# The seam before the up-projection of a decoder layer on one Trainium2 core: buffers of the first weight pairs exchanged, the last rows handled ahead of splits, one operand split by halves, gate sums in two groups

## The chip, the cores and the metric

The kernel runs on one core of a Trainium2 chip. A core has five engines that work side by side and meet through semaphores: TensorE (PE in the profile), VectorE (DVE), ScalarE (ACT), GpSimd (POOL) and SyncE (SP), which here issues most of the loads. The metric is the device time of one execution in microseconds (us). The kernel before took 1789.0, 1787.13 and 1788.75 us in three runs, a median of 1788.75.

## What is computed

One layer of a decoder trunk in float32, 1024 tokens of width 1024. Three branches (a recurrence, an attention, a cross-attention) are gated, projected and added to `x`; a feed-forward block with a causal convolution of width 3 follows. Cut to what matters here:

```python
def conv_ffn(x, g, w_up, conv_w, conv_b, w_down):
    h = rms_norm(x, g) @ w_up
    t = h.shape[1]
    hp = jnp.pad(h, ((0, 0), (CONV_W - 1, 0), (0, 0)))
    acc = conv_b + hp[:, 0:t] * conv_w[0]
    for i in range(1, CONV_W):
        acc = acc + hp[:, i:i + t] * conv_w[i]
    gate, val = jnp.split(acc, 2, axis=-1)
    return (jax.nn.silu(gate) * val) @ w_down

def reference(x, ...):
    ...
        x = x + merged @ w_out[l]
        x = x + conv_ffn(x, norm2_g[l], w_up[l], conv_w[l], conv_b[l], w_down[l])
    return x
```

`w_up` is 1024 x 5632 (2816 gate and 2816 value columns), `w_down` 2816 x 1024.

## The kernel before

**Matmuls in parts.** Each float32 operand is split into a high part (`hi`, a copy on ACT in a narrower form) and a low part (`lo`, what the copy lost, a subtraction). A product is then the sum of three: high times high, high times low, low times high. So each operand costs one ACT instruction and one subtraction, on DVE or POOL, before PE can use it. In `hl` (weights) the copy is line 1483 and the subtraction, always on POOL, line 1486. For the activations they are lines 1391 (ACT) and 1396 (DVE, or POOL where `eng=nc.gpsimd` is given). On PE all these matmuls are line 119, and the plain ones and the transposes line 105.

**Seven products for eight.** The up-projection multiplies 2 x 2 blocks of `w_up` with 2 x 2 blocks of the normed activations in Winograd's form: seven products in place of eight, of sums and differences of blocks. A product is four contraction tiles of 128 by three combinations of parts: 12 matmuls of 128 x 128 by 128 x 512, in one PSUM bank. Its activation sides have the names `11`, `21`, `22`, `T4`, `T1`, `T2`, `T3`, for the products 1 to 7 in this order (`side`, line 1468). Each side is two tiles (halves of the contraction, `j` = 0 and 1), each in a high and a low part. In the profile, the sides are `B` (11, 21, 22) and `BT` (T1 to T4), the tensors that they are split from `A`, `raw` and `t`.

**The seam.** `out_proj` computes `x + merged @ w_out` by row tiles of 128 tokens, norms each (`norm`: line 1342 loads the rows of x, 1347 adds, 1348 squares, 1354 scales), transposes it (`spread`, line 105) and forms the sums of blocks (`sums`, line 1378). The last row tile, the seventh, is left to `up_phase`, which does the first products between the pieces that still lack it. `old` is the part of a side that the first three of four row tiles of a half fill (384 of 512 columns), `new` the last 128. A split over both contraction halves of `old` has 768 elements to a partition in a tile, one of `new` 256.

**Pairs.** `w_up` is worked off in 22 pairs of blocks, gate and value columns in turn. Two tiles of 128 x 1024 are loaded for a pair by `load(n)` (line 1479), in buffers with the tag `rw` for even pairs and `wr` for odd ones, two buffers each; `t2`, the tensor from which the side T2 is split, lies in the buffers `wr` until it is split. `prep1`, `prep2` and `prep3` form the weight sides on POOL: sums of the blocks (lines 1505, 1506, 1518, 1519) and the splits by `hl`. Pair 0's weights are loaded and partly split earlier (`early`, the names `wsec`, `wsum`, `qk`).

**Products and what follows them.** `step(n, i)` does product i of pair n, and what reads its bank: `p1` is a copy of product 1's bank (line 1585), lines 1608, 1617, 1618, 1627 and 1634 on DVE add or subtract banks into the tiles `u`, which hold the up-projection with two columns of padding. `step(0, ..)` of product 7 is written out at lines 1696 to 1700. `conv` does the convolution on ACT (line 1552) and DVE (1553, 1554), and the gate: a sigmoid on ACT (1557) and products on DVE (1558 for the gate columns, 1563 for the value columns, which give `gall`). After each value pair, `act_sums` forms the sums that the down-projection's seven products need: two sums with `late` false and two with `late` true, all at line 1571, and sends `gall` and the sums to the DRAM tensor `actd` from ACT's queue (lines 1576, 1580, 1581).

**What sets the order.** PE's instructions, and all that is wrapped in `pinned` or `keep_in_program_order`, stay in the order in which the code writes them; the rest is placed by a scheduler with its own estimates, engine by engine. On the chip each engine then works strictly in its order.

The order of the products at the seam is (0,1), (1,1), the transposes of the last row tile, (0,2), (1,2), (0,5), (0,6), (0,7), (0,4), (0,3), where (n,i) is pair n's product i. Then come (1,6), (1,5), (1,4), (1,7), (2,1), (1,3), for pair 2 the products 5, 6, 2, 7, 4, 3, and for each later pair 1, 5, 6, 2, 7, 4, 3. Products 5 and 3 of a pair add into one bank, so do 6 and 7, and 1 and 2: before product 3 starts, DVE must have read product 5's sum (line 1618; 1700 for pair 0). Pair 3's product 1 follows (2,3). It is the down-projection (`down_phase`) that ends the kernel; its first loads take the buffers `rw` (`draw`) and `wr`.

Of the kernel before, what the change touches and what calls it, by code (L numbers as in the profile page):

```python
# [15 lines left out]
ALU = mybir.AluOpType  # L16
# [4 lines left out]
C = 64  # L21
# [28 lines left out]
class Trunk:  # L50
# [1407 lines left out]
    def up_phase(self, raws, t2, operand, split_hi, split_lo, sums, norm, spread):  # L1458
        nc = self.nc
        old, new = slice(0, 384), slice(384, 512)  # L1460
# [9 lines left out]
        pairs = [(o + 2 * f, f, o > 0) for f in range(NF // 2) for o in (0, NF)]  # L1470
        W, st = {}, {}

        def load(n):
            if n < len(pairs):
                tag, m = ("rw", pairs[n][0]) if n % 2 == 0 else ("wr", pairs[n][0])
                pool = self.pool_r if n % 2 == 0 else self.pool_wt
                W[n] = [pool.tile([128, 1024], F32, name=self.nm(tag), tag=tag, bufs=2) for _ in range(2)]
                for i in range(2):
                    nc.sync.dma_start(W[n][i], self.I["w_up"][m + i])

        def hl(src, pool, tags, n=1024, keep=False, queue=False):
            hi, lo = (pool.tile([128, n], F32R, name=self.nm(t), tag=t, bufs=16 if t == "l4" else 2) for t in tags)
            ins = nc.scalar.activation(hi, src, AF.Copy)  # L1483
            if keep:
                self.pinned(ins)
            ins = nc.gpsimd.tensor_tensor(lo, src, hi.bitcast(F32), ALU.subtract)  # L1486
            if queue:
                self.tc.keep_in_program_order(ins)
            return hi, lo

        L, R = slice(0, 512), slice(512, 1024)
# [5 lines left out]
        def prep2(n):  # L1497
            if n == 0:
                w = self.early[1]
            else:  # L1500
                w1, w2 = W[n]
                s = self.t4("it")
                st[n, "s"] = s
                fix = self.tc.keep_in_program_order if n == 2 else lambda ins: ins
                fix(nc.gpsimd.tensor_tensor(s[:, L], w2[:, L], w2[:, R], ALU.add))
                fix(nc.gpsimd.tensor_tensor(s[:, R], s[:, L], w1[:, L], ALU.subtract))
                w = hl(s, self.pool_l, ("l4", "l4"))
            st[n, 5], st[n, 6] = [[x[:, c] for x in w] for c in (L, R)]

        def prep3(n):  # L1510
            if n == 0:
                w2, s4 = self.early[2], self.early[3][:, R]
            else:
                w1, w2 = W.pop(n)
                s = st.pop((n, "s"))
                s4 = self.pool_r.tile([128, 512], F32, name=self.nm("s4"), tag="s4", bufs=1)
                fix = self.tc.keep_in_program_order if n == 1 else lambda ins: ins
                fix(nc.gpsimd.tensor_tensor(w2[:, L], w1[:, L], w2[:, L], ALU.subtract))
                fix(nc.gpsimd.tensor_tensor(s4, w1[:, R], s[:, R], ALU.subtract))
            w = hl(w2, self.pool_wt, ("wh", "wl"), keep=n == 1, queue=n == 1)  # L1520
            st[n, 7], st[n, 4] = [[x[:, c] for x in w] for c in (L, R)]
            if n == 1:
                return s4
            if n:
                st[n, 3] = hl(s4, self.pool_l, ("l4", "l4"), 512)
# [21 lines left out]
        L2, R2 = slice(2, 514), slice(514, 1026)  # L1547
# [35 lines left out]
        def evacuate(n):  # L1583
            p1 = st[n, "p1"] = self.r4("p1", n=512)
            ins = nc.scalar.activation(p1, st[n, "A"], AF.Copy)
            if n < 2:
                self.pinned(ins)

        def step(n, i):
# [10 lines left out]
            elif i == 5:  # L1600
                C = st[n, "C"] = bank()
                product(n, 5, C, True, True)
            elif i == 6:
# [3 lines left out]
                    st[n, "u1"] = u_tile()  # L1607
                self.pinned(nc.vector.tensor_tensor(st[n, "u1"][:, R2], Bk, st[n, "p1"], ALU.add))
                if n and pairs[n - 1][2]:
                    if n == 2:  # L1610
                        act_sums(pairs[n - 1][1], False)
                    act_sums(pairs[n - 1][1], True)
            elif i == 7:
                Bk = st.pop((n, "B"))
                product(n, 7, Bk, False, True)
                v = st[n, "u2"] = u_tile()
                nc.vector.tensor_tensor(v[:, L2], Bk, st.pop((n, "p1")), ALU.add)
                nc.vector.tensor_tensor(v[:, R2], st[n, "C"], v[:, L2], ALU.add)
            elif i == 40:
                Dk = st[n, "D"] = bank()  # L1620
                product(n, 4, Dk, True, True)
# [32 lines left out]
        prep1(1)  # L1654
        hi("22", old)
        hi("T1", old, (0,))
        hi("T2", old)
        next(norm)
        lo("T1", old, (0,))
        next(norm)  # L1660
        hi("T1", old, (1,))
        lo("T2", old)
        lo("22", old, eng=nc.gpsimd)
        step(0, 1)
        evacuate(0)
        next(norm, None)
        st[1, "A"] = bank()
        product(1, 1, st[1, "A"], True, True)
        spread()
# [4 lines left out]
        lo("T1", js=(1,))  # L1674
        hi("T2", new)
        lo("T2", new)
        load(1)
        step(0, 2)
        hi("T3", old)
        step(1, 2)  # L1680
        prep3(0)
        sums(384, 512, (1,))
        lo("T3", old)
        hi("T3", new)
        lo("T3", new)
        hi("22", new)
        lo("22", new, eng=nc.gpsimd)
        operand("T4", self.pool_a, "A", bufs=4)
        hi("T4")
        lo("T4")  # L1690
        prep2(0)
        st[0, 3] = hl(self.early[3][:, R], self.pool_l, ("l4", "l4"), 512, True)
        step(0, 5)
        prep2(1)
        step(0, 6)
# [370 lines left out]
```

## Time and profile before

| | us |
|---|---|
| median of three runs | 1788.75 |
| the profiled execution | 1788.76 |
| its span, first to last instruction | 1787.0 |
| PE busy (10479 matmuls) | 1771.8 |
| DVE busy | 1181.5 |
| ACT busy | 865.3 |
| POOL busy | 792.5 |
| mean granted clock of PE | 0.999 |

The profile is one execution, recorded by the hardware. Busy time is that in which an engine works on an instruction. PE is the engine that is hardly ever idle, so time goes where PE waits or where the clock granted to it is below 1. In the rows, `L1396` is a line of the kernel, `out<-in` are the program's names without their numbers, `128x512` a tile's partitions and elements, `x4` the number of instructions in a group. The bracket `[0.90 <-DVE BT L1396]` says that the engine stood idle for 0.90 us before this row, and what let it go.

### The profile page before, as it was taken

What the parts mean: (1) busy time and instruction counts of PE and PEld (TensorE: products, weight loads), DVE (VectorE), ACT (ScalarE), POOL (GpSimd) and SP (SyncE); (2) the same over time, 40 slices, a digit from 0 to 9 for tenths busy, and PEclk for the clock granted to TensorE, in tenths of its full rate; (3) what the DMA queues carried; (4) which work ended last, traced back from release to release, by engine and by line L of the source; (5) the groups of instructions that cost most, each with busy time, mean ns of one, the idle gap of its engine ahead of it and who ended that gap; (6) DMA issues with size and microseconds to landing.
All of it is one profiled execution on the core that took longest, in us unless ns stands there. A gap on an engine that the chain in (4) does not pass through costs nothing.

```text
span 1787.0 us, 27327 instructions
## 1 busy us (share of the span) xinstructions
PE 1771.8 (99%) x10479; PEld 1440.1 (81%) x10479; DVE 1181.5 (66%) x1604; ACT 865.3 (48%) x1566; POOL 792.5 (44%) x448
## 2 busy tenths in 40 slices
PE   9999999999999999999999999999999999999999
PEld 7777778888888888777777888878888888888887
DVE  5667774898988624234443962687767777795597
ACT  6544343656666635534444334544444445454343
POOL 3223352331231453122332542487677677545454
PEclk9999999999999999999999999999999999999999
DMA  5145565111112443568554553223323323386476
GB/s 210 60 161 182 179 224 163 51 54 57 54 57 77 127 120 95 212 226 282 201 190 177 203 186 110 103 99 103 111 89 99 119 90 121 126 317 220 146 239 209
DMA packets 122771, 261.28 MB, mean 146 GB/s; under 512 B 28681, under 2 KB 43657, under 8 KB 122514
## 3 DMA queue, kind: packets, MB, share of 16 engines
q1 hardware_dynamic: 85026, 193.83, 32.9%
q10 hardware_dynamic: 33840, 53.10, 8.1%
q0 software_dynamic: 3776, 12.62, 2.4%
q8 instruction: 82, 1.34, 0.3%
q14 instruction: 47, 0.39, 0.1%
HBM read 178.99 MB, written 80.48 MB: 145 GB/s over the span
## 4 chain that ended last, share of the span: by engine, by line
PE 81%; DVE 6%; POOL 2%; issue 1%; ACT 1%; DMA 1%; DVEq 0%; SPq 0%; POOLq 0%; ACTq 0%
PE mm L119 66%; PE g L119 12%; PE g L105 3%; DVE it L554 1%; DVE at L939 1%; DVE inst L556 1%; DMA A<-yd 1%; POOL wl L1486 0%; DVE gall L1571 0%; DMA scr<-at 0%; POOL hf L781 0%; DVE w L344 0%; POOL l L1486 0%; DVE w L834 0%; DVE qk L877 0%
## 5 line engine op out<-in xcount | busy, mean ns | idle before, releaser
L81 POOL TENSOR_TENSOR wl<-wr,wh 128x1024 fp32r<-128x1024 f32 (+2 forms) x78 | 197.1, 2527 | 468.0 <-ACT wh L80 465.0
L119 PE MATMUL mm<-xhi,wh 128*128 128x512 f32 x784 | 260.3, 413 | 0.5 <-DVE w L331 0.4
L119 PE MATMUL mm<-xlo,wh 128*128 128x512 f32 x784 | 243.6, 392 | 0.0
L119 PE MATMUL mm<-xhi,wl 128*128 128x512 f32 x784 | 242.5, 391 | 0.0
L119 PEld LDWEIGHTS mm<-xlo,wh 128*128 128x128 f32 x784 | 147.1, 188 | 33.3 <-DVE xlo L208 0.4
L119 PEld LDWEIGHTS mm<-xhi,wl 128*128 128x128 f32 x784 | 147.0, 188 | 33.1 <-POOL wl L81 0.7
L119 PEld LDWEIGHTS mm<-xhi,wh 128*128 128x128 f32 x784 | 136.7, 190 | 28.9 <-issue 6.1
L80 ACT ACTIVATE wh<-wr 128x1024 fp32r<-128x1024 f32 (+2 forms) x78 | 81.8, 1049 | 130.9 <-PE mm L119 100.1
L119 PE MATMUL mm<-dw,da 128*128 128x512 f32 x528 | 120.3, 389 | 0.0
L119 PE MATMUL mm<-BT,l 128*128 128x512 f32 x504 | 118.0, 389 | 1.4 <-POOL l L1486 1.4
L1775 POOL TENSOR_TENSOR dw<-draw,dw 128x512 fp32r<-128x512 f32 x55 | 82.6, 1511 | 75.7 <-ACT dw L1773 70.0
L119 PEld LDWEIGHTS mm<-dw,da 128*128 128x128 f32 x528 | 99.1, 188 | 20.6
L119 PEld LDWEIGHTS mm<-BT,l 128*128 128x128 f32 x504 | 94.5, 188 | 21.5 <-POOL l L1486 1.8
L119 PE MATMUL mm<-BT,wh 128*128 128x512 f32 x352 | 108.7, 389 | 0.9 <-DVE BT L1396 0.9
L119 PE MATMUL mm<-B,wh 128*128 128x512 f32 x352 | 108.8, 390 | 0.0
L939 DVE TENSOR_TENSOR_SCAN at<-at,nrt 128x128 f32<-128x128 f32 (+3 forms) x64 | 96.3, 1514 | 18.2 <-ACT at L933 18.0
L1774 DVE TENSOR_TENSOR da<-draw,da 128x512 fp32r<-128x512 f32 x77 | 64.2, 839 | 51.5 <-ACT da L1772 51.2
L1486 POOL TENSOR_TENSOR l<-it,l 128x1024 fp32r<-128x1024 f32 x21 | 50.9, 2422 | 90.2 <-ACT l L1483 90.1
L119 PE MATMUL g<-dw,da 128*128 128x512 f32 x396 | 90.2, 389 | 0.0
L119 PEld LDWEIGHTS g<-dw,da 128*128 128x128 f32 x396 | 74.3, 188 | 15.4
L1772 ACT ACTIVATE da<-draw 128x512 fp32r<-128x512 f32 x77 | 48.2, 628 | 78.5 <-PE mm L119 32.0
L834 DVE TENSOR_TENSOR w<-w,nrt 128x1024 f32<-128x1024 f32 x24 | 46.6, 1941 | 57.3 <-ACT w L833 46.4
(337 smaller groups left out, 3979.2 us busy)
## 6 DMA issues: line engine op xcount, KB each, us to landing
wr<-in_w_in_dram SPq DMA_DIRECT2D x48, 512.0 KB, 3.6
draw<-actd SPq DMA_DIRECT2D x77, 256.0 KB, 2.9
draw<-in_w_down_dram SPq DMA_DIRECT2D x55, 256.0 KB, 4.6
at<-scr SPq DMA_DIRECT2D x24, 512.0 KB, 6.0
wr<-in_w_up_dram SPq DMA_DIRECT2D x22, 512.0 KB, 3.5
actd<-gall ACTq DMA_DIRECT2D x44, 256.0 KB, 3.2
rw<-in_w_up_dram SPq DMA_DIRECT2D x20, 512.0 KB, 3.5
gsd<-w ACTq DMA_DIRECT2D x18, 512.0 KB, 3.0
```

The lines of the kernel that those rows point to most:

```text
L80: (fix_hi or fix)(self.nc.scalar.activation(hi, raw, AF.Copy))
L81: fix(self.nc.gpsimd.tensor_tensor(lo, raw, hi.bitcast(F32), ALU.subtract))
L105: self.pinned(self.nc.tensor.transpose(out, in_, self.ident[:n, :n]))
L119: self.pinned(self.nc.tensor.matmul(*a, **k))
L554: self.pinned(nc.vector.tensor_tensor(tv, X[:, 0:s, s : s + 1].to_broadcast([128, s, n]), X[:, s : s + 1, s + 1 : 64].to_broadcast([128, s ...
L556: self.pinned(nc.vector.tensor_tensor(X[:, 0:s, s + 1 : 64], X[:, 0:s, s + 1 : 64], tv, ALU.add))
L834: fix(nc.vector.tensor_tensor(g, g, self.nrb, ALU.mult))
L939: self.pinned(nc.vector.tensor_tensor_scan(sn[:, :W][:, ::-1], sn[:, :W][:, ::-1], self.nrt[:, 1152 - W :][:, ::-1], 1.0, ALU.mult, ALU.max))
L1486: ins = nc.gpsimd.tensor_tensor(lo, src, hi.bitcast(F32), ALU.subtract)
L1772: self.pinned(nc.scalar.activation(A[:, 0], a, AF.Copy))
L1774: self.pinned(nc.vector.tensor_tensor(A[:, 1], a, A[:, 0].bitcast(F32), ALU.subtract))
L1775: nc.gpsimd.tensor_tensor(Wt[:, 1], w, Wt[:, 0].bitcast(F32), ALU.subtract)
```

## The change

All edits are in `up_phase`. The even pairs now have the buffers `wr` and the odd ones `rw`; pair 1 is loaded earlier, in `rw`, in the order of the program. The last row tile's squares and scaling stand ahead of several splits, whose halves are reordered. T3's low parts are split half by half. The low half of `wsum` and pair 1's sums come in a fixed order on POOL. After pair 2's product 6 only two gate sums of pair 1 are done; the other two come behind the second addition after pair 2's product 7.

```diff
         def load(n):
             if n < len(pairs):
-                tag, m = ("rw", pairs[n][0]) if n % 2 == 0 else ("wr", pairs[n][0])
-                pool = self.pool_r if n % 2 == 0 else self.pool_wt
+                tag, m = ("wr", pairs[n][0]) if n % 2 == 0 else ("rw", pairs[n][0])
+                pool = self.pool_wt if n % 2 == 0 else self.pool_r
                 W[n] = [pool.tile([128, 1024], F32, name=self.nm(tag), tag=tag, bufs=2) for _ in range(2)]
                 for i in range(2):
-                    nc.sync.dma_start(W[n][i], self.I["w_up"][m + i])
+                    ins = nc.sync.dma_start(W[n][i], self.I["w_up"][m + i])
+                    if n == 1:
+                        self.pinned(ins)
...
-                fix = self.tc.keep_in_program_order if n == 2 else lambda ins: ins
+                fix = self.tc.keep_in_program_order if n < 3 else lambda ins: ins
...
-            w = hl(w2, self.pool_wt, ("wh", "wl"), keep=n == 1, queue=n == 1)
+            w = hl(w2, self.pool_wt, ("wh", "wl"), keep=n < 2, queue=n < 2)
...
                 if n and pairs[n - 1][2]:
-                    if n == 2:
-                        act_sums(pairs[n - 1][1], False)
-                    act_sums(pairs[n - 1][1], True)
+                    act_sums(pairs[n - 1][1], n > 2)
             elif i == 7:
...
-                nc.vector.tensor_tensor(v[:, R2], st[n, "C"], v[:, L2], ALU.add)
+                ins = nc.vector.tensor_tensor(v[:, R2], st[n, "C"], v[:, L2], ALU.add)
+                if n == 2:
+                    self.pinned(ins)
+                    act_sums(pairs[n - 1][1], True)
...
         hi("T1", old, (0,))
-        hi("T2", old)
         next(norm)
+        load(1)
         lo("T1", old, (0,))
+        hi("T2", old, (0,))
         next(norm)
-        hi("T1", old, (1,))
-        lo("T2", old)
+        lo("T2", old, (0,))
         lo("22", old, eng=nc.gpsimd)
         step(0, 1)
+        next(norm, None)
+        hi("T2", old, (1,))
         evacuate(0)
-        next(norm, None)
+        hi("T1", old, (1,))
+        lo("T2", old, (1,))
         st[1, "A"] = bank()
...
-        load(1)
         step(0, 2)
+        prep3(0)
         hi("T3", old)
         step(1, 2)
-        prep3(0)
         sums(384, 512, (1,))
-        lo("T3", old)
         hi("T3", new)
-        lo("T3", new)
+        for j in range(2):
+            for ts in (old, new):
+                lo("T3", ts, (j,))
         hi("22", new)
         lo("22", new, eng=nc.gpsimd)
         operand("T4", self.pool_a, "A", bufs=4)
+        st[0, 3] = hl(self.early[3][:, R], self.pool_l, ("l4", "l4"), 512, True, True)
         hi("T4")
         lo("T4")
         prep2(0)
-        st[0, 3] = hl(self.early[3][:, R], self.pool_l, ("l4", "l4"), 512, True)
         step(0, 5)
```

The order of PE's instructions is the same before and after. The places that matter are on DVE and POOL. In these rows an instruction stands with its line, its operation, out<-in and its tile; lines behind 1479 have moved by two or three numbers in the kernel after.

On DVE, the low parts of T3 and then of T4. `BT_1_0_10523` and `BT_1_1_10524` are T3's low parts for the contraction halves 0 and 1, of `old` (384 columns) and `new` (128); `BT_1_0_10667` and `BT_1_1_10668` are T4's. The difference, with + for the kernel after:

```order
 L1396 TENSOR_TENSOR BT_1_0_10523<-A_9819,BT_0_0_10521 128x2x384
+L1396 TENSOR_TENSOR BT_1_0_10523<-A_9819,BT_0_0_10521 128x2x128
 L1396 TENSOR_TENSOR BT_1_1_10524<-A_9820,BT_0_1_10522 128x2x384
-L1396 TENSOR_TENSOR BT_1_0_10523<-A_9819,BT_0_0_10521 128x2x128
 L1396 TENSOR_TENSOR BT_1_1_10524<-A_9820,BT_0_1_10522 128x2x128
 L1396 TENSOR_TENSOR BT_1_0_10667<-raw_9818,BT_0_0_10665 128x1024
 L1396 TENSOR_TENSOR BT_1_1_10668<-raw_9818,BT_0_1_10666 128x1024
```

The first half's second piece has moved ahead of the second half's first piece.

On DVE, the gate sums between the two products 6 and 7 of pair 2; L1608, L1617, L1618 and L1627 are the reads of PSUM banks described above, and before stands:

```order
L1544 MEMSET u_10957 128x2
L1608 TENSOR_TENSOR u_10957<-mm_10944,p_1643_10891 128x512
L1571 TENSOR_TENSOR gall<-gall 128x512 x4
L1544 MEMSET u_11005 128x2
L1617 TENSOR_TENSOR u_11005<-mm_10944,p_1643_10891 128x512
L1618 TENSOR_TENSOR u_11005<-mm_10927,u_11005 128x512
L1627 TENSOR_TENSOR u_11005<-u_11005,mm_11009 128x512
L1553 SCALAR_TENSOR_TENSOR g_11024<-u_11005,params,g_11024 128x512
L1553 SCALAR_TENSOR_TENSOR g_11030<-u_11005,params,g_11030 128x512
```

and after, where the lines behind 1618 are three further down and the sums are at L1573:

```order
L1546 MEMSET u_10957 128x2
L1610 TENSOR_TENSOR u_10957<-mm_10944,p_1643_10891 128x512
L1573 TENSOR_TENSOR gall<-gall 128x512 x2
L1546 MEMSET u_11001 128x2
L1617 TENSOR_TENSOR u_11001<-mm_10944,p_1643_10891 128x512
L1618 TENSOR_TENSOR u_11001<-mm_10927,u_11001 128x512
L1573 TENSOR_TENSOR gall<-gall 128x512 x2
L1630 TENSOR_TENSOR u_11001<-u_11001,mm_11009 128x512
L1637 TENSOR_TENSOR u_10957<-mm_10927,u_10957 128x512
L1555 SCALAR_TENSOR_TENSOR g_11024<-u_11001,params,g_11024 128x512
```

Of the four sums two now stand behind L1618, and the addition behind product 3 (L1637, before L1634) stands ahead of the convolution.

On POOL, from pair 0's split of `wsec` to pair 1's sums (`wsum` is pair 0's too; `it`, `s` and the raw weights `wr` or `rw` are pair 1's; `B` is side 22's low part); before:

```order
L1486 TENSOR_TENSOR wl_10648<-wsec_10307,wh_10647 128x1024
L1396 TENSOR_TENSOR B_1_0_10511<-A_9821,B_0_0_10509 128x2x128
L1396 TENSOR_TENSOR B_1_1_10512<-A_9822,B_0_1_10510 128x2x128
L1505 TENSOR_TENSOR it_10690<-wr_10612 128x512
L1506 TENSOR_TENSOR it_10690<-it_10690,wr_10611 128x512
L1486 TENSOR_TENSOR l_1607_10674<-wsum_10308,l_1606_10673 128x512
L1486 TENSOR_TENSOR l_1611_10694<-it_10690,l_1610_10693 128x1024
L1518 TENSOR_TENSOR wr_10612<-wr_10611,wr_10612 128x512
L1519 TENSOR_TENSOR s_1619_10755<-wr_10611,it_10690 128x512
L1486 TENSOR_TENSOR wl_10759<-wr_10612,wh_10758 128x1024
```

and after:

```order
L1488 TENSOR_TENSOR wl_10631<-wsec_10307,wh_10630 128x1024
L1396 TENSOR_TENSOR B_1_0_10511<-A_9821,B_0_0_10509 128x2x128
L1396 TENSOR_TENSOR B_1_1_10512<-A_9822,B_0_1_10510 128x2x128
L1488 TENSOR_TENSOR l_1607_10670<-wsum_10308,l_1606_10669 128x512
L1507 TENSOR_TENSOR it_10690<-rw_10539 128x512
L1508 TENSOR_TENSOR it_10690<-it_10690,rw_10538 128x512
L1488 TENSOR_TENSOR l_1611_10694<-it_10690,l_1610_10693 128x1024
L1520 TENSOR_TENSOR rw_10539<-rw_10538,rw_10539 128x512
L1521 TENSOR_TENSOR s_1619_10755<-rw_10538,it_10690 128x512
L1488 TENSOR_TENSOR wl_10759<-rw_10539,wh_10758 128x1024
```

The low half of `wsum` stands ahead of the two sums `it`, and the sums read `rw` in place of `wr`. On SP the load of the last rows of `x` (L1342) now stands ahead of the first of the two loads into the next pair's weight buffers, where it stood behind it.

## The prediction

> **What bounds the kernel now.** The page's first part gives PE 1771.8 of 1787.0 us busy, so a change can only win where PE stands still. The view of waits, kept to PE, has only five of them in the stretch that the diff touches; its columns are the waiting engine and line, the releaser, total, count, longest.
>
> ```profile
> PE mm L119 <- DVE u L1618: 2.2, 1, 2.2
> PE mm L119 <- POOL l L1486: 1.4, 1, 1.4
> PE mm L119 <- DVE BT L1396: 0.9, 1, 0.9
> PE g L105 <- ACT sq L1354: 0.6, 1, 0.6
> PE mm L119 <- ACT l L1483: 0.4, 1, 0.4
> ```
>
> The timeline of PE sets them in time: start, duration, line, tile, shape, count, and in brackets the idle time with its releaser.
>
> ```profile
> 1163.18 0.39 PE L119 MATMUL mm<-BT,wh 128*128 128x512 f32 x1
> 1164.47 0.50 PE L119 MATMUL mm<-BT,wh 128*128 128x512 f32 x1 [0.90 <-DVE BT L1396]
> ...
> 1186.83 2.88 PE L119 MATMUL mm<-B,l 128*128 128x512 f32 x12
> ...
> 1191.59 5.32 PE L119 MATMUL mm<-BT,l 128*128 128x512 f32 x22 [1.42 <-POOL l L1486]
> ...
> 1204.68 0.39 PE L119 MATMUL mm<-BT,wl 128*128 128x512 f32 x1
> 1207.30 4.32 PE L119 MATMUL mm<-B,l 128*128 128x512 f32 x12 [2.23 <-DVE u L1618]
> 1211.42 0.92 PE L119 MATMUL mm<-B,wh 128*128 128x512 f32 x2
> 1212.17 0.40 PE L119 MATMUL mm<-B,wl 128*128 128x512 f32 x1
> ...
> 1214.48 2.88 PE L119 MATMUL mm<-BT,l 128*128 128x512 f32 x12
> ```
>
> A product is 12 matmuls. At 1186.83 they take 2.88, the last of them 0.39, so one starts every (2.88 - 0.39) / 11 = 0.227 us and a product takes 2.72. At 1207.30 a product takes 4.12 (to 1211.42), and the next 3.06 (to 1214.48): 1.40 + 0.34 = **1.74 us lost to the clock**. The windows of PE (stretch, its length, busy time with count, granted clock, DMA share, GB/s) show it:
>
> ```profile
> 1207.00:1208.00 1.00, 0.70 (x3) 1.00 0.68 258
> 1209.00:1210.00 1.00, 1.00 (x4) 0.50 0.00 0
> ```
>
> So the change plays for 5.6 us of waits (2.2 + 1.4 + 0.9 + 0.6 + 0.4, rounded values) and 1.74 of slow clock; each wait also costs some 0.2 us more than its figure (1164.47 - 1163.18 - 0.23 = 1.06 for the 0.90). That makes about 8.4 us at most, 1780.4. The times of before are those of the profiled execution, 1788.76 (span 1787.0 and 1.76 around it), which is the median, 1788.75, to 0.01.
>
> **The last rows of x.** Start, duration and line again, of SP, DVE, ACT and PE:
>
> ```profile
> 1141.84 0.43 SPq L1342 DMA_DIRECT2D x<-in_x_dram  x1
> 1146.29 1.29 DVE L1347 TENSOR_TENSOR x<-mm,x 128x512 f32<-128x512 f32 x2 [0.45 <-DMA x<-in_x_dram]
> 1150.12 1.15 ACT L1354 ACTIVATE sq<-x,ss 128x1024 f32<-128x1024 f32 x1 [0.54 <-POOL ss L180]
> 1150.29 0.39 PE L119 MATMUL mm<-B,wl 128*128 128x512 f32 x1
> 1151.32 1.09 PE L105 MATMUL g<-kon,sq 128*128 128x128 f32 x8 [0.65 <-ACT sq L1354]
> ```
>
> The transposes start at 1151.32 and could at 1150.52 (1150.29 + 0.23): 0.80. The load no longer stands behind a weight load on SP, and DVE waits for it 0.45 us; the squares and the scaling on ACT now also stand ahead of T2's and T1's splits. 0.45 of an earlier load and about 0.4 of reordering cover it: **-0.80** (bounds 0 and -0.80). It is worth something only if what follows is earlier too.
>
> **T3 by halves, and POOL beside it.** Rows of DVE, then POOL:
>
> ```profile
> 1147.50 0.95 DVE L1396 TENSOR_TENSOR BT<-raw,BT 128x768 fp32r<-128x768 f32 x1
> 1159.85 0.41 DVE L1378 TENSOR_TENSOR A<-A,A 128x256 f32<-128x256 f32 x1
> 1161.19 3.56 DVE L1396 TENSOR_TENSOR BT<-A,BT 128x768 fp32r<-128x768 f32 x4
> 1164.68 3.44 DVE L1396 TENSOR_TENSOR BT<-raw,BT 128x1024 fp32r<-128x1024 f32 x2
> ```
> ```profile
> 1161.77 2.37 POOL L1396 TENSOR_TENSOR B<-A,B 128x256 fp32r<-128x256 f32 x2 [2.12 <-ACT B L1391]
> 1165.47 1.56 POOL L1505 TENSOR_TENSOR it<-wr 128x512 f32<-128x512 f32 x1 [1.34 <-DMA wr<-in_w_up_dram]
> 1167.11 2.16 POOL L1506 TENSOR_TENSOR it<-it,wr 128x512 f32<-128x512 f32 x1
> 1169.24 1.28 POOL L1486 TENSOR_TENSOR l<-wsum,l 128x512 fp32r<-128x512 f32 x1
> ```
>
> T3's four low parts (768, 768, 256, 256 elements) take 3.56 where 0.95 and 0.41 apiece would give 2.72. The first half needs the third of them now and will need the second: the 0.90 (1.06 with its edge) goes for that matmul. But the rows show a second thing: **an elementwise DVE instruction with all operands in SBUF and a POOL instruction hold each other up**. The sum `it` at 1167.11 takes 2.16 beside a split of DVE, and a POOL instruction of that shape takes 1.28 when DVE works from PSUM (1169.24). The Trainium skill, SBUF — State Buffer, section "Who interferes with whom", says that the loser of the port pair which the two share is blocked wholly, not slowed; the rows agree (2.16 against 1.28), and without that rule the sum would be the third rival's.
>
> Before, POOL stood idle 1.34 us here for the load into `wr`. Now pair 1 is in `rw`, loaded early, and the low half of `wsum` is ahead of the sums: POOL has three instructions ready as soon as its two splits `B` are done, just when DVE has four of six pieces left. The six alone are 2 x 0.95 + 2 x 0.41 + 2 x 1.27 (an estimate, 0.95 x 4/3) = 5.3; from 1161.19 they ended at 1168.12 (1164.68 + 3.44), 6.9 later. With five POOL instructions between them (about 0.6 of each `B`, 1.28 + 1.30 + 1.30) they take up to 5.3 + 5.1 = 10.4. Less the 0.80 of an earlier start, T4's last piece is done between 1167.3 (as before) and 1170.8; I take 1169.4, since most of the instructions ready will take turns: **+1.3** for T4. So PE loses about 0.9 to 1.3 us at each of T3's second half, T4's two halves and product (0,3): the waits are spread out, not gone.
>
> **What follows 1:1.** ACT and POOL, the chain behind T4:
>
> ```profile
> 1178.63 1.20 ACT L1557 ACTIVATE sg<-g 128x512 f32<-128x512 f32 x2 [1.71 <-DVE g L1554]
> 1180.42 1.30 POOL L1486 TENSOR_TENSOR l<-s,l 128x512 fp32r<-128x512 f32 x1 [1.71 <-ACT l L1483]
> 1208.15 4.74 POOL L1486 TENSOR_TENSOR wl<-wr,wh 128x1024 fp32r<-128x1024 f32 x2
> ```
>
> The convolution of pair 0 (DVE L1553, L1554) comes behind T4's pieces on DVE, ACT's gates behind it, ACT's `l<-s` behind those, and POOL waits for that at 1180.42. From there POOL never stops until the stretch ends, so its 1.3 goes straight through: product (2,5), which waits for POOL at 1191.59, starts at 1192.9 (**+1.3**).
>
> **Gate sums by twos.** DVE:
>
> ```profile
> 1198.93 6.88 DVE L1571 TENSOR_TENSOR gall<-gall 128x512 f32<-128x512 f32 x4
> 1206.46 0.69 DVE L1618 TENSOR_TENSOR u<-mm,u 128x512 f32<-128x512 f32 x1
> 1238.56 1.42 DVE L1571 TENSOR_TENSOR gall<-gall 128x512 f32<-128x512 f32 x2
> ```
>
> Beside POOL the four sums take 1.72 each (alone 0.71, at 1238.56), and L1618, which reads the bank into which product (2,3) adds, stands behind all four. Two of them go behind it: 3.4 earlier, against the 2.39 that PE lost (1207.30 - 1204.68 - 0.23). So that wait goes: product (2,3) starts at 1191.59 + 1.3 + 13.3 = 1206.2 (13.3 from 1191.59 to 1204.91) and ends at 1208.9. A sum moved behind L1618 delays L1627 by 1.4 to 3.4; that costs PE nothing, since its reader, the convolution, has no PE work behind it for several products, and 1.4 to 3.4 if that cover were gone.
>
> **What is late next.** Product (3,1) takes its low weights from the first of the two `wl` splits at 1208.15, which ends at half of 4.74, 1210.5; its third matmul needs them and ran at 1212.17, behind the slow clock. Now the split ends at 1210.5 + 1.3 = 1211.8, and PE comes to that matmul at 1208.9 + 0.45 = 1209.4: **a new wait of about 2.5 us**, on POOL in place of DVE. Behind it on PE stand the rest of (3,1) and the products 5 and 6 of pair 3; ACT's copy of (3,1)'s bank waits with them, and nothing that PE needs in the next two products waits for that copy. Ten matmuls later, at 1211.8 + 2.3 = 1214.1, the product is done, against 1214.48: the sum is **-0.3** where the clock stays full, 1788.4. With the slow clock again, 1.74 on top: **+1.4**, 1790.2.
>
> Which? A 2.23 us wait dropped the clock to 0.50; a 1.42 us wait did not. A 2.5 us wait is nearest to the first. Of the three times shown, 1789.0, 1787.13 and 1788.75, one is lower by 1.6 to 1.9, the size of the 1.74: I read it as a run without the drop, so two runs in three have it, and a median has it likelier still. The Trainium skill, TensorE: Matmul & The Clock Gate, section "What's actually happening", has the clock fall only after an idle window of about 3.4 us, and by that neither wait would touch it: the sum would be 1788.4. The trace disagrees with its 0.50 after 2.23 us.
>
> **At nothing.** The exchange of `rw` and `wr` in the later pairs moves no wait of PE; at the end the first loads of the down phase wait for pair 21's splits, at the latest as the two `wr` loads did before, and their first reader comes 18 us later (1573.80 - 1549.99 - 5.82). That is the cover, and what they'd cost beyond it is their lateness.
>
> ```profile
> 1549.99 5.82 SPq L1749 DMA_DIRECT2D wr<-in_w_down_dram  x2
> 1573.80 6.51 PE L119 MATMUL mm<-dw,da 128*128 128x512 f32 x28
> ```
>
> **Rivals.**
> - Forecast, 46%: POOL's split takes DVE's place and the clock drops: 1790.2 (1789.5 to 1791.5).
> - Same wait, clock full, 23%: 1788.4. For it: one of three runs, the 1.42 wait; against: the row of 0.50.
> - DVE and POOL take fewer turns, 20%: T4 is done up to 1.9 sooner than before (5.3 from 1160.9, which is 1161.19 less part of the 0.80, to 1166.2), so all behind it too: third matmul of (3,1) at 1210.5 - 1.9 = 1208.6, product done 1210.9, -3.6 with a full clock: 1785.2; with the drop 1786.9. Against: 2.16 and 1.72 in the rows.
> - POOL's split is in time as well and all waits go, 5%: 1780.4 to 1784. Against: POOL has no idle time from 1180.42 on.
> - Slower, 6%: the turns cost more than my 10.4 allows (each T4 piece also behind ACT's high part). It decides at T4 done 3.4 later than before, 1171.5: -0.3 + 2.1 + 1.74 = +3.5; at 1172.2, 1793.
> - The change doesn't do what it says: if the sums stay late, PE waits for DVE as now and 1.3 later, 1790.0: inside the forecast.
>
> **How the numbers follow.** 1790.2 is the likeliest. The range leaves out the case in which all goes and the slower one: 1785.2 to 1791.8. Faster by over 0.2% (3.6 us, about what a measurement of this kernel tells from no change), under 1785.2: the 5%, and a third of the third: 0.12. Slower, over 1792.3: 0.06. Within: 0.82.
>
> **What would show it.** The list of PE's waits loses DVE L1618 and ACT sq, and gains POOL `wl` at 2 to 3 us near 1209; DVE BT waits several times for about 1 us; POOL's `l<-s` near 1180.4 stands about 1.3 later; the window behind the new wait shows 0.50. Wrong would be: `l<-s` earlier than 1180 (third rival), no wait of PE on POOL (fourth), or one on another line.

## The result, and the profile after

| | before | after |
|---|---|---|
| median of 17 runs, us | 1788.02 | 1790.83 |
| lowest and highest | 1786.24, 1790.78 | 1789.56, 1793.19 |
| ratio, 95% interval | | 1.0016 (1.0009 to 1.0022) |
| profiled execution (span) | 1788.76 (1787.0) | 1793.19 (1791.4) |

The kernel is slower by 1.6 to 3.9 us (0.09% to 0.22% of 1788): the change moves time rather than saving any. The profiled execution of after happens to be the slowest of the 17, so its rows need a correction, which comes below.

The list of PE's waits, after (in all, times, longest; groups of under 0.7 us left out, and those outside the seam but for the one on L1610):

```profile
PE mm L119 <- POOL wl L1488: 2.5, 1, 2.5
PE mm L119 <- DVE BT L1396: 2.3, 3, 1.2
PE mm L119 <- DVE u L1610: 1.9, 1, 1.9
...
PE mm L119 <- POOL l L1488: 1.5, 1, 1.5
...
PE mm L119 <- DVE u L1706: 0.7, 1, 0.7
```

ACT's `sq` and DVE's L1618 are gone; POOL's `wl`, two more waits on `BT`, one on L1706 and one on L1610 have come. PE's timeline sets them in time:

```profile
1149.53 0.39 PE L119 MATMUL mm<-B,wl 128*128 128x512 f32 x1
1149.76 1.03 PE L105 MATMUL g<-kon,sq 128*128 128x128 f32 x8
...
1164.93 0.49 PE L119 MATMUL mm<-BT,wh 128*128 128x512 f32 x1 [1.17 <-DVE BT L1396]
1167.16 0.50 PE L119 MATMUL mm<-BT,wh 128*128 128x512 f32 x1 [0.57 <-DVE BT L1396]
1169.39 0.50 PE L119 MATMUL mm<-BT,wh 128*128 128x512 f32 x1 [0.57 <-DVE BT L1396]
...
1206.11 2.88 PE L119 MATMUL mm<-B,l 128*128 128x512 f32 x12
1211.90 0.50 PE L119 MATMUL mm<-B,wl 128*128 128x512 f32 x1 [2.45 <-POOL wl L1488]
1215.62 5.88 PE L119 MATMUL mm<-BT,l 128*128 128x512 f32 x24
...
1359.77 0.72 PE L119 MATMUL mm<-BT,wh 128*128 128x512 f32 x2 [1.89 <-DVE u L1610]
```

The transposes follow the matmul before them without a gap (1149.76 - 1149.53 = 0.23). Product (2,3) starts at 1206.11 at full speed. Product (3,1) then waits 2.45 us for POOL, and the window behind it has the clock at half:

```profile
1213.00:1215.00 2.00, 2.00 (x6) 0.50 0.74 246
```

Rows of DVE, then of POOL, for the other end of the chain:

```profile
1157.00 2.63 DVE L1378 TENSOR_TENSOR raw<-t,raw 128x256 f32<-128x256 f32 x1
...
1160.22 4.66 DVE L1396 TENSOR_TENSOR BT<-A,BT 128x768 fp32r<-128x768 f32 x4
1164.80 4.53 DVE L1396 TENSOR_TENSOR BT<-raw,BT 128x1024 fp32r<-128x1024 f32 x2
```
```profile
1156.72 2.63 POOL L1488 TENSOR_TENSOR wl<-wsec,wh 128x1024 fp32r<-128x1024 f32 x1 [3.70 <-ACT wh L1485]
...
1162.60 1.99 POOL L1488 TENSOR_TENSOR l<-wsum,l 128x512 fp32r<-128x512 f32 x1
1164.56 1.46 POOL L1507 TENSOR_TENSOR it<-rw 128x512 f32<-128x512 f32 x1
1166.10 2.15 POOL L1508 TENSOR_TENSOR it<-it,rw 128x512 f32<-128x512 f32 x1
...
1181.65 1.29 POOL L1488 TENSOR_TENSOR l<-s,l 128x512 fp32r<-128x512 f32 x1 [1.70 <-ACT l L1485]
```

The six pieces on DVE now take from 1160.22 to 1169.33 (1164.80 + 4.53), 9.1 us in place of 6.9; between them stand POOL's three, each slower than the 1.3 us that such an instruction takes without DVE beside it. `l<-s`, which starts POOL's long stretch, is at 1181.65 against 1180.42.

**Where the profile's 4.4 us lie.** PE's instructions have the same order in both, so their starts can be set against each other. At the matmul ahead of the transposes after is 0.76 us *ahead* (1149.53 against 1150.29); that difference arose far ahead of the seam, where both kernels issue the same work. At the end of product (3,1) after is 1.14 behind (1215.62 against 1214.48): the seam costs **1.9** to that point, and 0.27 more within the next products, whose first matmuls still run with the slow clock. At 1224 another 0.4 comes, behind a gate product on DVE that waits for ACT until 1222.94; at 1359.77 there are 2.2, and some 0.4 near the end. The 2.2 are not the seam's, as the last section shows.

### The profile page after: what moved, and what is told of

Read it like the earlier page. It is cut to its first block, busy times and chain, and to the rows that moved or that the text cites. A ratio compares the mean times of both kernels' runs of the same rounds, so it can differ in the third digit from the quotient of the medians.

```text
span 1791.4 us, 27323 instructions
## 1 busy us (share of the span) xinstructions
PE 1772.0 (99%) x10479; PEld 1439.2 (80%) x10479; DVE 1183.7 (66%) x1604; ACT 864.1 (48%) x1566; POOL 792.8 (44%) x448
## 4 chain that ended last, share of the span: by engine, by line
PE 79%; DVE 6%; POOL 3%; issue 2%; ACT 1%; DMA 1%; DVEq 0%; POOLq 0%; SPq 0%; ACTq 0%
PE mm L119 64%; PE g L119 12%; PE g L105 3%; POOL l L1488 1%; DVE it L554 1%; DVE at L939 1%; DVE inst L556 1%; POOL wl L1488 1%; DMA A<-yd 1%; POOL it L1507 0%; DMA scr<-at 0%; POOL it L1508 0%; POOL hf L781 0%; DVE w L344 0%; DVE w L834 0%
## 5 line engine op out<-in xcount | busy, mean ns | idle before, releaser
L1554 ACT ACTIVATE g<-u,params 128x512 f32<-128x512 f32 x88 | 65.1, 770 | 40.4 <-DVE u L1637 24.0
```

Source lines behind the costliest of these rows:

```text
L1554: nc.scalar.activation(c, u[:, 2 + h * 512 : 514 + h * 512], AF.Identity, scale=self.par("cw2", m), bias=self.par("cb", m))
```

## The experiments

The ratio of each is to the kernel before, run beside it.

**Gate sums alone.** The kernel before with this edit only:

```diff
-                    if n == 2:
-                        act_sums(pairs[n - 1][1], False)
-                    act_sums(pairs[n - 1][1], True)
+                    act_sums(pairs[n - 1][1], n > 2)
...
-                nc.vector.tensor_tensor(v[:, R2], st[n, "C"], v[:, L2], ALU.add)
+                ins = nc.vector.tensor_tensor(v[:, R2], st[n, "C"], v[:, L2], ALU.add)
+                if n == 2:
+                    self.pinned(ins)
+                    act_sums(pairs[n - 1][1], True)
```

> The kernel before, with the gate sums by twos and nothing else of the change. Theory (DVE's place is taken by POOL): the 2.2 us wait on L1618 goes, and product (3,1) waits about 2.4 us for the first of pair 3's splits on POOL, which ends at about 1210.5 as before; product (3,1) ends 0 (clock at 0.50 again) to 1.6 us (clock full) sooner: ratio to the kernel before 0.9990 to 1.0002. Rival (the gate sums were the whole loss and POOL is in time): 4 us less, ratio 0.9978. Rival (the gate sums are what makes the change slower): ratio 1.001 or more.

Measured: 1.0006 (0.9998 to 1.0015), no difference that the interval can tell. PE's timeline:

```profile
1210.04 0.79 PE L119 MATMUL mm<-B,wl 128*128 128x512 f32 x1 [2.51 <-POOL wl L1486]
```

The DVE wait of 2.23 us went and one of 2.51 on POOL took its place. The ratio is a little over the theory's 1.0002, which lies inside its interval. The rival of 4 us less is out; the one of 1.001 or more is not excluded by the interval, but no row speaks for it: the only new wait stands in the place of the old one.

**Gate sums undone.** The change without that edit (the diff above, backwards).

> The whole change with the four gate sums back ahead of L1618. Theory: T4 is done as late as in the changed kernel (about 1.2 us behind the kernel before, 1.9 against the entry into the seam), POOL's split at 1180 with it, so the sums on DVE start at 1200.1 and L1618 is done at about 1208.5; PE waits there some 2.2 us with the slow clock behind it, and the POOL split at 1211.9 is hidden: the end is within 0.5 us of the changed kernel, ratio to the kernel before 1.0013 to 1.0020. Rival (the turns of DVE and POOL at T4 cost nothing, the sums do): ratio 0.9995 to 1.0003.

Measured: 1.0014 (1.0005 to 1.0023), within the theory's range. PE waits 2.28 us for the read behind the four sums; the slow clock that was expected behind it did not come in the profiled execution (1.00). So the slowness comes with the rest of the change, not with the sums.

**Buffers back.** The change with `rw` and `wr` as before:

```diff
-                tag, m = ("wr", pairs[n][0]) if n % 2 == 0 else ("rw", pairs[n][0])
-                pool = self.pool_wt if n % 2 == 0 else self.pool_r
+                tag, m = ("rw", pairs[n][0]) if n % 2 == 0 else ("wr", pairs[n][0])
+                pool = self.pool_r if n % 2 == 0 else self.pool_wt
```

> The whole change with the buffers as before: pair 1 in wr, pair 2 in rw; the load of the last rows stands behind an rw load again. Theory: POOL waits for the wr load again and takes fewer turns with DVE, so T4 is done about 1168.1 or earlier, PE's waits at T3 and T4 shrink, and POOL's split for product (3,1) comes about 1.5 us sooner than in the changed kernel: ratio to the kernel before 0.9998 to 1.0008. Rival (the exchange costs nothing; the order of POOL and the halves do): ratio 1.0015.

Measured: 1.0019 (1.0010 to 1.0028). The theory missed: POOL's rows are those of after, to the hundredth in duration.

```profile
1162.40 1.99 POOL L1488 TENSOR_TENSOR l<-wsum,l 128x512 fp32r<-128x512 f32 x1
1164.36 1.46 POOL L1507 TENSOR_TENSOR it<-wr 128x512 f32<-128x512 f32 x1
1165.90 2.15 POOL L1508 TENSOR_TENSOR it<-it,wr 128x512 f32<-128x512 f32 x1
```

With `l<-wsum` ahead of the sums, the load into `wr` is there before POOL comes to them. The exchange neither causes the turns nor costs anything that shows; that is the rival.

**T3 whole.** The change with T3's low parts in the old order:

```diff
+        lo("T3", old)
         hi("T3", new)
-        for j in range(2):
-            for ts in (old, new):
-                lo("T3", ts, (j,))
+        lo("T3", new)
```

> The whole change with T3's low parts in the old order (768, 768, 256, 256 elements). Theory: the halves only move the wait inside product (0,7): its second matmul waits about 1.4 us in place of none, its seventh about 0.2 in place of 1.2, and T4's last piece is done at 1169.3 as in the changed kernel, so nothing behind changes: ratio to the kernel before 1.0010 to 1.0020. Rival (the halves cause the extra turns with POOL): T4 done 1 us or more earlier, ratio 1.0006 or less.

Measured: 1.0018 (1.0010 to 1.0027), as the theory has it. PE waits 1.44 us at the second matmul of product (0,7), in place of 1.17 at the seventh, and T4's pieces end at 1169.22 (1164.69 + 4.53). The halves are worth nothing here.

**The high half of `wsum` behind T4's.** One ACT instruction moved back, the only difference to after:

```diff
-        st[0, 3] = hl(self.early[3][:, R], self.pool_l, ("l4", "l4"), 512, True, True)
         hi("T4")
+        st[0, 3] = hl(self.early[3][:, R], self.pool_l, ("l4", "l4"), 512, True, True)
         lo("T4")
```

> The whole change with one ACT instruction moved: the high half of wsum behind T4's high parts, as before the change. POOL's order is kept, so POOL waits for it and starts its three instructions at about 1164.7 in place of 1162.6. Theory (turns of DVE and POOL make T4 late): DVE's T3 pieces run alone, T4's last piece is done at about 1167.1 in place of 1169.3, POOL's split at 1181.65 comes about 2 us sooner, and with it product (2,5) and (3,1): 2 us less than the changed kernel, ratio to the kernel before 1.0000 to 1.0010. Rival (what is late at T4 is PE or ACT, or POOL's work only moves into the next stage): ratio 1.0013 to 1.0020.

Measured: 1.0005 (0.9996 to 1.0014), within the theory's range. DVE, then POOL:

```profile
1159.89 3.57 DVE L1396 TENSOR_TENSOR BT<-A,BT 128x768 fp32r<-128x768 f32 x4
1163.38 3.45 DVE L1396 TENSOR_TENSOR BT<-raw,BT 128x1024 fp32r<-128x1024 f32 x2
```
```profile
1164.35 1.39 POOL L1488 TENSOR_TENSOR l<-wsum,l 128x512 fp32r<-128x512 f32 x1 [2.05 <-ACT l L1485]
...
1179.66 1.29 POOL L1488 TENSOR_TENSOR l<-s,l 128x512 fp32r<-128x512 f32 x1 [1.70 <-ACT l L1485]
```

POOL waits 2.05 us for the high half, DVE's six pieces take 6.9 us again (1159.89 to 1166.83), and `l<-s` comes 2.0 us sooner than in after (1.7 if the entries, 0.3 apart, are set against each other). The median is 1.7 us below that of after, and the rival's least ratio, 1.0013, lies at the very end of the interval, so it is nearly but not wholly excluded: by the medians, this place in the order of two engines is most of what the change costs.

**Pair 3's splits first.** Now the wait on POOL at product (3,1). Pair 3's splits and pair 4's sums are held in the order of the program:

```diff
-            w = self.early[4 * n] if n < 2 else hl(W[n][0], self.pool_wt, ("wh", "wl"), keep=n == 2, queue=n == 2)
+            w = self.early[4 * n] if n < 2 else hl(W[n][0], self.pool_wt, ("wh", "wl"), keep=n in (2, 3), queue=n in (2, 3))
...
-                fix = self.tc.keep_in_program_order if n < 3 else lambda ins: ins
+                fix = self.tc.keep_in_program_order if n < 5 else lambda ins: ins
```

> The whole change, and pair 3's splits on POOL ahead of pair 4's three sums (an order held by the program for pairs 3 and 4). Theory: the split that product (3,1) waits for starts at about 1204.9 in place of 1209.5 and ends at about 1207.3, ahead of PE's arrival at 1209.1, so the 2.45 us wait and the slow clock behind it (1.6) go: 4 us less than the changed kernel, ratio to the kernel before 0.9992 to 0.9996. Rival (something else is late within a microsecond, such as DVE's convolution or pair 4's own splits): ratio 1.0005 to 1.0015.

Measured: 1.0010 (1.0001 to 1.0019): the rival. The 2.45 us wait went, and PE ran straight into another one, at product (3,7); PE, then DVE, then ACT:

```profile
1222.29 0.74 PE L119 MATMUL mm<-BT,wh 128*128 128x512 f32 x2 [2.27 <-DVE u L1546]
```
```profile
1220.93 0.69 DVE L1560 TENSOR_TENSOR gall<-g,sg 128x512 f32<-128x512 f32 x1 [3.42 <-ACT sg L1559]
```
```profile
1219.36 1.06 ACT L1485 ACTIVATE l<-it 128x1024 fp32r<-128x1024 f32 x1 [3.23 <-POOL it L1508]
1220.32 0.58 ACT L1559 ACTIVATE sg<-g 128x512 f32<-128x512 f32 x1
```

Read backwards: DVE's bank read (L1610, named here by the `MEMSET` beside it) stood behind a gate product, that behind a sigmoid on ACT, that behind a high part of pair 4, and that waited for a sum on POOL. It is POOL again, by three engines. But POOL wasn't short of time there: ahead of these sums it had stood idle for 5.74 us, to 1213.05, for the high part of pair 3's second tile on ACT.

**The gate products behind the read.** As the former, and pair 2's last gate products (with `pinned`) are issued after product (3,6)'s read:

```diff
-                if (n, i) == (0, 0):
+                if (n, i) in ((0, 0), (2, 0)):
                     return gates
...
+                elif (n, i) == (3, 6):
+                    for close in st.pop((2, "gates")):
+                        close()
```

> As the experiment with pair 3's splits first, and pair 2's last two gate products on DVE behind the read of product (3,6)'s bank in place of ahead of it. In the former the 2.45 us wait on POOL went, and a wait of 2.27 us for DVE at product (3,7) came: DVE's gate product waited 3.4 us for a sigmoid that stands on ACT behind pair 4's high part. Theory: without that the PE wait at product (3,7) goes as well: 2.2 to 2.6 us less than the former (1.0010), ratio to the kernel before 0.9994 to 1.0000. Rival (yet another engine is late, such as POOL's or DVE's work for pair 3): ratio 1.0005 or more.

Measured: 1.0013 (1.0005 to 1.0022): the rival once more. The wait at (3,7) went, and product (4,1) waits:

```profile
1230.49 0.50 PE L119 MATMUL mm<-B,wl 128*128 128x512 f32 x1 [1.92 <-POOL wl L1488]
```

**The three edits together** (high half of `wsum`, pair 3's splits, gate products).

> The three edits together: high half of wsum behind T4's, pair 3's splits ahead of pair 4's sums, pair 2's last gate products behind the read of (3,6). Theory: their gains add, 2 and 4: about 6 us less than the changed kernel, ratio to the kernel before 0.9978 to 0.9990. Rival (the first stage is made up by the second, since PE's waits there only move): ratio as the second experiment of this call.

Measured: 1.0000 (0.9991 to 1.0009), 3 us below after, half of what was expected: product (4,1) still waits 1.96 us for POOL. By the profiles the loss is all there: set against the entry, this kernel is 3.85 us ahead of before at the end of product (3,1), but only 1.60 ahead after product (4,1). POOL:

```profile
1203.13 2.40 POOL L1488 TENSOR_TENSOR wl<-rw,wh 128x1024 fp32r<-128x1024 f32 x1
1211.27 2.41 POOL L1488 TENSOR_TENSOR wl<-rw,wh 128x1024 fp32r<-128x1024 f32 x1 [5.74 <-ACT wh L1485]
```

Between pair 3's two splits POOL again stands idle for 5.74 us, and the sums of pair 4 that product (4,1) needs stand behind the second. Whether filling that gap, without taking any work from POOL, would have been enough was not tried: the kernels below that fill it also have pair 2's sums on DVE.

**Work taken from POOL.** On top of the three edits, pair 2's four sums on DVE, in three places. First at once behind `prep1(2)`:

```diff
+            eng = nc.vector if n == 2 else nc.gpsimd
...
         prep1(2)
+        sums2(2)
+        sums3(2)
```

(`sums2` and `sums3` are the two pairs of sums out of `prep2` and `prep3`.)

> As the experiment with the three edits, and pair 2's four sums on DVE in place of POOL, issued where DVE is idle at about 1180 (DVE needs 0.7 us for one, POOL 1.3). Theory (POOL's time is what bounds the seam behind T4, so a wait that is removed without taking work from POOL only moves on): POOL is some 2.5 us ahead from pair 2's low halves on, the wait at product (2,5) (1.2 us) goes and the one at product (4,1) (2.0 us) shrinks or goes: 2 to 3 us less than the experiment with three edits, ratio to the kernel before 0.9982 to 0.9990. Rival (a sum on DVE blocks POOL as long as it saves there, or the delayed reads of banks cost PE the same): ratio 0.9996 or more.

Measured: 1.0017 (1.0008 to 1.0026). The waits on POOL shrank to 0.4 and 0.7 us, as expected, but the rival's number came, by its second reason: product (1,7) waits for the read of (1,6)'s bank, which now stands on DVE behind the sums:

```profile
1185.27 1.22 PE L119 MATMUL mm<-BT,wh 128*128 128x512 f32 x2 [4.37 <-DVE u L1622]
```

Then with pair 4's first sums between pair 3's two splits (`sums2(4)` behind `prep1(3)`):

> As the former, with pair 4's three sums on POOL between pair 3's first and second split, where POOL stood idle for 5.7 us waiting for ACT, in place of behind the second. Theory: POOL's work for pair 4 and 5 comes 4 us sooner, so product (4,1) waits for nothing; if the former still has that wait, 1 to 2 us less than the former, ratio 0.9976 to 0.9986; if it has not, equal to it. Rival (DVE's gate sums then collide with these sums, and L1618's reads come late): ratio above the former's by 0.0005 or more.

Measured: 1.0016 (1.0007 to 1.0025). The wait of 0.7 at (4,1) went; the 4.4 stayed, and the ratio is that of the former within the noise. Then with the sums of pair 2 behind that read (`(n, i) == (1, 6)`):

> As the former experiment, with pair 2's four sums on DVE behind the read of product (1,6)'s bank in place of ahead of it. In the former the waits on POOL behind (2,5) were gone or below 0.5 us, but product (1,7) waited 4.4 us for that read, which stood on DVE behind the four sums, and the clock fell to half behind it. Theory (POOL's time bounds the seam; the loss there was only the place of the sums): this wait and its slow clock go, 5 to 6 us less than the former, ratio to the kernel before 0.9975 to 0.9990. Rival (the sums are late anyway or block POOL, so that product (2,5) waits for POOL as before): ratio 0.9995 or more.

Measured: 1.0001 (0.9992 to 1.0010), the rival's number but not its reason: no wait on POOL came back (0.4 at most). Two of the sums took 2.88 us each between POOL's instructions, and the read for product (1,3) stood behind them; DVE, then PE:

```profile
1184.82 2.88 DVE L1514 TENSOR_TENSOR s<-wr,it 128x512 f32<-128x512 f32 x1
```
```profile
1189.69 4.61 PE L119 MATMUL mm<-B,l 128*128 128x512 f32 x12 [2.71 <-DVE u L1630]
```

Last, the latter two sums behind the reads of product (1,7), and the second of these reads held in the order of the program:

```diff
-                if n == 2:
+                if n < 3:
                     self.pinned(ins)
+                if n == 2:
                     act_sums(pairs[n - 1][1], True)
...
                 elif (n, i) == (1, 6):
                     sums2(2)
+                elif (n, i) == (1, 7):
                     sums3(2)
```

> As the former experiment, with only the first two of pair 2's four sums on DVE ahead of the reads behind product (1,7), and the other two behind them. In the former the four sums took 7.8 us between POOL's instructions, and PE waited 2.7 us at product (1,3) for the read behind them, with the slow clock after it (1.7). Theory (POOL's time bounds the seam, DVE has room, only the places of the sums were wrong): that wait and its slow clock go and no wait on POOL over 0.5 us comes back: 3 to 4.5 us less than the former, ratio to the kernel before 0.9975 to 0.9985. Rival (another wait takes its place once more, as in each step before): ratio 0.9992 or more.

Measured: **0.9985 (0.9976 to 0.9995)**, a median of 1785.35 against 1788.13, at the slower end of the theory's range: 2.8 us below the kernel before and some 5.5 below the change, the only version that is faster than both. What is left of PE's waits in the seam:

```profile
PE mm L119 <- DVE u L1622: 1.1, 1, 1.1
PE mm L119 <- DVE u L1719: 0.8, 1, 0.8
PE mm L119 <- DVE u L1630: 0.5, 1, 0.5
PE mm L119 <- POOL l L1488: 0.4, 1, 0.4
PE mm L119 <- DVE BT L1396: 0.3, 1, 0.3
```

Set against the entry, this kernel is 3.11 us ahead of before at the end of product (3,1), less than the 3.85 of the three edits alone, and still 3.11 after product (4,1): by the profiles it is faster than they are since it loses nothing there. It has both of what could do that, the sums on DVE and pair 4's sums in POOL's gap, and no run tells the two apart.

## Why the prediction was right, and where a size was off

- **The last rows of x:** -0.80 forecast, and the gap of 0.80 is gone. What was wrong is that I took the same 0.80 off for DVE's splits behind it. Set against the entry (0.76 ahead), DVE starts T3 only 0.2 sooner (1160.22 + 0.76 against 1161.19): a sum of blocks at 1157.00 took 2.63 us beside POOL's `wl<-wsec`, which took 2.63 from 1156.72. The gain ended at another such collision; before had it as well (two splits of DVE that took 2.97 from 1156.95, beside the same split of POOL at 1157.20), and against the entry that split of POOL stands 0.28 later now. The load counts for little in the 0.80: in the buffers-back kernel, where DVE waits 0.47 us for these rows as it did before, the gap is 0.23, so some 0.6 came from the order on ACT and DVE.
- **T4:** this is the term that was mis-sized. Forecast +1.3 for its last piece; +1.97 set against the entry (1169.33 + 0.76 against 1168.12). In the trace's own times the guess of 1169.4 was met, but only since that execution came to the seam 0.76 earlier. The six pieces take 9.1 us; full turns were put at up to 10.4, and the start 0.80 earlier. The mechanism is shown by the moved ACT instruction, which took 2.2 us off the six pieces and 1.7 off the median. The row at 1157.00 shows it at its plainest: an instruction of 0.41 us ended 0.28 us after POOL's had ended.
- **What makes the turns:** the prediction named the exchange of buffers beside the order. The buffers-back kernel, in which pair 1 is loaded as late as before (issued at 1159.52), shows that the order alone does it.
- **T3's waits spread out, not gone:** four waits, of 1.17, 0.57, 0.57 and 0.69, where 0.9 to 1.3 each was forecast; the kernel with T3 whole shows that the halves don't matter.
- **The 1:1 chain to POOL:** `l<-s`, product (2,5) and the split for product (3,1) are all later by what T4 is within 0.15 us: by 1.23, 1.20 and 1.36 in the trace's times, where T4 is 1.21 later, and 0.76 more each against the entry.
- **Gate sums and what is late next:** product (2,3) was forecast for 1206.2 and starts at 1206.11; the new wait was forecast at about 2.5 us near 1209 on POOL `wl` and is 2.45. The wait was right by its mechanism, since the split and PE's arrival both moved with T4; that 1206.2 was met is luck, as with T4's 1169.4: against the entry the product starts at 1206.87.
- **The clock:** it fell to 0.50 behind the wait, as in the likeliest case, which the prediction had at 46% against 23%. Over a whole run the mean clock is 0.999 in 11 of the 17 runs of after and 1.000 in 6, and these six are the six fastest (1789.56 to 1790.23). So it is right that some executions have the drop and others not.
- **The sum:** +1.4 with T4 at +1.3. With +2.0 it is +2.1, and the seam has 1.9 + 0.27 = 2.2. The median lies 2.8 above, with 1.6 to 3.9 as bounds. Of what is over, 0.4 is the delay at 1224, which the profiles of buffers back and T3 whole show too; where the rest lies isn't shown. That the time itself, 1790.83, is only 0.6 off the forecast 1790.2 is partly luck: the forecast was counted from 1788.75, the kernel before took 1788.02 beside the change, and the change in time is twice what was forecast. The fourth rival, in which all waits go, did not come: the wait that went ahead of product (2,3) came back at later products until the last of the experiments.

## What to carry to other kernels

When a wait of the bounding engine is removed, ask what is late next. Here POOL worked without a break from 1181.65 to 1211.85, so the wait for DVE that went at product (2,3) came back as one for POOL at (3,1), and when that one was removed by order, as others at (3,7) and then at (4,1). Look also for idle time of the engine that is late: POOL's 5.7 us between two splits stood unused while PE waited for it. When work is put on another engine, its place in that engine's order counts as much as its length: the same four sums gave 1.0016, 1.0001 and 0.9985, by which bank reads stood behind them. And an instruction that gets ready sooner isn't always better: POOL's early start beside DVE's splits cost 1.7 us, and a high half issued later gave it back.

## What the runs showed that was not expected

**The clock after a wait depends on where the wait falls.** Of 16 waits of PE between 1.9 and 2.7 us in these profiles, 10 had the granted clock at 0.50 behind them and 6 had not; a wait of 1.92 did it (pair 4's product, above) and waits of 2.27 and 2.48 didn't (the kernels with pair 3's splits first and with the moved ACT instruction). Both waits of 4.4 did. So the length alone doesn't settle it.

The traces' records of the clock show what does. Each of the ten drops lasts 3.41 us, and where an execution has two, their starts are a whole number of times 3.4133 us apart: 1213.08 and 1359.86 with buffers back (146.78, 43 times), 129.71 (38 times) with the gate products behind, 174.08 (51 times) in the first with sums on DVE. Now mark every execution off in windows of 3.4133 us that begin with its drops (where none came, with the first rise of the clock, 4 to 7 us after the start, which lies on the same marks: in after at 4.45, 354 windows ahead of the drop at 1212.77), and cut each wait where a window ends. All ten waits with a drop have a piece of 1.88 us or more in one window, and the clock falls at the end of that window; the longest piece of the six without is 1.74. The wait of 2.48 is cut into 1.42 and 1.06, the wait of 1.92 lies whole in one window. A wait of 4.38, cut into 2.06 and 2.32, lowered the clock for two windows, 6.83 us. So in these traces the clock fell when PE stood idle for about 1.8 us or more of a window. As an estimate from this, a wait of 2.45 us at a chance place has such a piece about two times in three, which fits the 11 of 17 runs.

The Trainium skill, TensorE: Matmul & The Clock Gate, section "What's actually happening", calls the window free-running: that fits a drop that depends on where a wait falls, while its idle window of about 3.4 us is longer than the waits that sufficed here.

**A DMA issue on ACT that takes 0.3 or 2.6 us.** The 2.2 us at 1359.77 come from ACT's queue, about 10 us earlier; after:

```profile
1349.31 2.63 ACTq L1578 DMA_DIRECT2D actd<-gall  x2
```

The second of the two issues took 2.03 us there, and ACT's work behind it, with DVE's behind that, came later. The rest is DVE and POOL in turns again: the two gate sums ahead of L1610 now fall beside a split of POOL. After, DVE and POOL, then before, DVE:

```profile
1355.58 3.53 DVE L1573 TENSOR_TENSOR gall<-gall 128x512 f32<-128x512 f32 x2
1356.17 2.38 POOL L1488 TENSOR_TENSOR l<-it,l 128x1024 fp32r<-128x1024 f32 x1 [5.31 <-ACT l L1485]
```
```profile
1352.80 1.42 DVE L1571 TENSOR_TENSOR gall<-gall 128x512 f32<-128x512 f32 x2
```

Before, the two sums were done ahead of POOL's split at 1354.37. In the 14 profiles the same issue took 0.33 to 2.61. In the five with 2.03 or more PE waited 1.9 to 2.4 us for L1610 (or its like) at this place; in the nine with 1.87 or less it didn't. The kernels with such an issue are after, buffers back, gate products behind, `wsum` moved and the first with sums on DVE; the kernel before had 1.06. What makes the issue long was not tried, so whether the change makes it more frequent is open.
